# An attention stage's entries listed one by one, W_o split without GpSimd and late, and the last output on two queues

## The chip, the core and the metric

The kernel runs on one core of one Trainium2 chip. The metric is the device time of one execution in microseconds; the time before is the median of three runs. One execution was also taken by the hardware profiler, and all lines of the profile and the trace come from it.

## The reference

A decoder trunk of two layers over 256 positions of width 1024, in fp32. Layer 0 mixes positions with a gated linear recurrence, layer 1 with attention. Around each mixer stand two SwiGLU blocks of inner width 2816, and every part ends in a normalisation and a residual sum. The change touches layer 1's attention and the kernel's last output:

```python
q = (xq @ w_q).reshape(Bn, S, N_HEADS, HEAD_DIM).transpose(0, 2, 1, 3) * (HEAD_DIM ** -0.5)
for blk in range(S // Q_BLOCK):            # two blocks of 128 queries
    logits = jnp.einsum('bhqd,bhkd->bhqk', q[:, :, q0:end], k[:, :, :end])
    logits = logits + c[:, :, q0:end, None] - c[:, :, None, :end]
    logits = jnp.where(kpos[None, :] <= qpos[:, None], logits, -jnp.inf)
    p = jax.nn.softmax(logits, axis=-1)
    outs.append(jnp.einsum('bhqk,bhkd->bhqd', p, v[:, :, :end]))
...
return o @ w_o
...
h = h + rms_norm(m, mix_post_g[layer])
f = swiglu(rms_norm(h, ffn2_pre_g[layer]), ffn2_w_gate[layer], ffn2_w_up[layer], ffn2_w_down[layer])
h = h + 0.5 * rms_norm(f, ffn2_post_g[layer])
```

There are 16 heads of 64. The first block of queries looks at 128 keys, the second at 256.

## The kernel before

The 256 positions are two tiles of 128, t=0 and t=1. The residual stream `h[t]` stays in the core's memory; the weights are streamed from device memory once. TensorE (PE) follows the order of the program. The other engines, VectorE (DVE), ScalarE (ACT), GpSimd (POOL) and the DMA queue of SyncE (SP), get their order from a planner that works ahead of the run; `tc.high_priority()` favours instructions, and `tc.keep_in_program_order` pins one at its place in the program.

**Products in three passes.** Each fp32 operand is held as a high part in the format fp32r and a rest. `mm3` (lines 185 to 187) multiplies high by high, high by rest and rest by high into one PSUM bank.

**Units.** Weights come in units of 128 x 1024 numbers (512 KB). `load_raw` issues the transfer on SP's queue into one of five `raw` buffers; `split` makes `whi` (a cast) and `wlo` (raw minus `whi`), each with nine buffers. Normally ACT casts (line 174) and DVE subtracts (line 179). For every second unit of W_o (`dve=True`, odd k), DVE casts (line 172) and POOL subtracts.

**Items, slots and ticks.** `items` lists the units in the order of use, each with `prep` (load and split) and `work(t, u)` (the products of one tile). `slot(t, i)` runs the work and then a `tick`. A tick runs deferred steps that are due (`defer(n, fn)` waits for n further ticks) and calls `prepare_next`, which emits the load and split of the next unit, if the unit nine places earlier is finished by both tiles and an estimate of the transfer allows it. `half(t, i)` is a slot that afterwards sets `state["a"]` (t=0) or `state["b"]` (t=1) to the number of items that the tile has passed.

**The attention stage** begins at item `n_ffn3`: eight units of W_q (two column halves n of four units each), then eight of W_o (k = 0 to 7). A slot of either is six matmuls of 128x512. At the end of a column half, `heads_T` scales q into `htok` (DVE, line 921); two ticks later PE transposes it (line 926), and ACT (line 929) and DVE (line 930) each copy half of the heads into `qT`. Two more rows of `qT` come by small transfers on POOL's queue (`att_rows`, lines 914 and 915), which also loads the table for the exponential.

`attention(t)` works in groups of heads: four groups of four heads for t=0, eight groups of two for t=1. Each group has four operations:

- `logits`: matmuls (line 1030), then mask and maximum on DVE (1031, 1033), then exponentials with their sum on ACT (1038)
- `norm`: reciprocal and scaling of the probabilities `pe` on DVE (1044, 1045)
- `turn`: four transposes on PE (1051), copy to `pT` on ACT (1053)
- `values`: eight matmuls (1065); after each half of the heads, `oh` on ACT (1071) and `ol` on DVE (1072)

They are put together in steps: step i holds norm(i−1), logits(i), values(i−3) and turn(i−2). The order of the stage is written out by hand in `ATT_ORDER`: "0" or "1" is a slot of that tile, "a0" or "a1" the next step of that tile's attention. W_o's products for t=0 stand between the steps of t=1. After the last W_o slot, `enter` adds the normalised result to `h[t]` and prepares the input of the SwiGLU block that follows.

**The end.** `enter(..., last=True)` finishes the last block. For t=1 it cuts `h` into four pieces of 256 columns: three are one DVE instruction each (line 286) and leave on SP's queue; the first is scaled on ACT (288), added on POOL (289) and leaves on ACT's queue (line 291 issues all).

Of the kernel before, what the change touches and what calls it, by code (L numbers as in the profile page):

```python
# [9 lines left out]
F32 = mybir.dt.float32  # L10
F32R = mybir.dt.float32r
BF16 = mybir.dt.bfloat16
AF = mybir.ActivationFunctionType
ALU = mybir.AluOpType
# [30 lines left out]
def trunk_kernel(ctx: ExitStack, tc: tile.TileContext, A: dict, out: bass.AP):  # L45
# [108 lines left out]
    def load_raw(src, parts, n, pieces=1):  # L154
        v = new_raw()[:parts, :n]
        if len(src.shape) == 3:
            a, m = src.shape[1] // pieces, n // pieces
            for c in range(pieces):
                nc.sync.dma_start(v[:, c * m:(c + 1) * m].rearrange("p (a b) -> p a b", a=a),
                                  src[:, c * a:(c + 1) * a, :])  # L160
        else:
            nc.sync.dma_start(v, src)
        return v

    def split(rawv, parts, n, pieces=1, dve=False):
        u = Unit()
        hi = wpool.tile([P, 1024], F32R, tag="whi", name=nm("whi"), bufs=WB)
        lo = wpool.tile([P, 1024], F32R, tag="wlo", name=nm("wlo"), bufs=WB)
        m = n // pieces
        for c in range(0, n, m):  # L170
            if dve:
                nc.vector.tensor_copy(hi[:parts, c:c + m], rawv[:, c:c + m])
            else:
                up = nc.scalar.activation(hi[:parts, c:c + m], rawv[:, c:c + m], AF.Copy)  # L174
                if settled[0]:
                    tc.keep_in_program_order(up)
                    settled[0] = False
            low = nc.gpsimd if dve else nc.vector
            low.tensor_tensor(lo[:parts, c:c + m], rawv[:, c:c + m], hi[:parts, c:c + m].bitcast(F32), ALU.subtract)  # L179
        u.hi, u.lo = hi[:parts, :n], lo[:parts, :n]  # L180
        return u

# [78 lines left out]
    def enter(t, dests, pf, gb, half, last=False, normed=False):  # L261

        f = 1.0 / 16 if half else 1.0 / 32
        ss = new_ss()
        t1 = []
        urgent = tc.high_priority()
        urgent.__enter__()
        for n in range(2):
            square_sum(pf[n], ss[:, n:n + 1], f)
        for n in range(2):  # L270
            if n == 1 and last:
                r = rstd_of(ss, 2, f, nc.vector)
            t1.append(hpool.tile([P, 512], F32, tag="t1", name=nm("t1"), bufs=2))
            nc.vector.tensor_tensor(t1[n], pf[n], gb[:, n * 512:(n + 1) * 512], ALU.mult)  # L274
        if not last:
            r = rstd_of(ss, 2, f)

        ve, po, sp, aq = nc.vector, nc.gpsimd, nc.sync, nc.scalar
        pieces = [(n * 512, 512, ve, None) for n in range(2)]
        if last:  # L280
            pieces = ([(0, 256, ve, sp), (256, 256, ve, sp), (512, 512, ve, sp)] if t == 0 else
                      [(0, 256, po, aq), (256, 256, ve, sp), (512, 256, ve, sp), (768, 256, ve, sp)])
        for c, m, en, q in pieces:
            hn, tn = h[t][:, c:c + m], t1[c // 512][:, c % 512:c % 512 + m]
            if en is ve:
                en.scalar_tensor_tensor(hn, tn, r[:, 0:1], hn, ALU.mult, ALU.add)
            else:
                nc.scalar.activation(tn, tn, AF.Copy, scale=r[:, 0:1])
                en.tensor_tensor(hn, tn, hn, ALU.add)
            if last:  # L290
                q.dma_start(out[0, t * P:(t + 1) * P, c:c + m], hn)
        urgent.__exit__(None, None, None)
        if last:
            return

        def inputs():
            tps = [to_tp(h[t], n) for n in range(2)]
            for dest in dests:
                to_x(tps, dest)
            stat(t)  # L300

        def norm():
            with tc.high_priority():
                normed_x()

        def normed_x():
            ss = new_ss()
            for n in range(2):
                square_sum(h[t][:, n * 512:(n + 1) * 512], ss[:, n:n + 1])
            rs[t] = rstd_of(ss, 2)  # L310
            hn = []
            for n in range(2):
                hn.append(hpool.tile([P, 512], F32, tag="t1", name=nm("hn"), bufs=2))
                nc.vector.tensor_scalar(hn[n], h[t][:, n * 512:(n + 1) * 512], rs[t][:, 0:1], None, ALU.mult)

            def go():
                tps = []
                for n in range(2):
                    tp = gtbank()
                    for j in range(4):  # L320
                        nc.tensor.transpose(tp[:, j * P:(j + 1) * P], hn[n][:, j * P:(j + 1) * P], ident)
                    tps.append(tp)
                to_x_tiles(tps, dests[0])
            defer(6, go)

        if normed:
            norm()
            settled[0] = True
        else:
            defer(3, inputs)  # L330
# [14 lines left out]
    first_acc = []  # L345
    landed = {}

    def prepare_next(must=False):

        i = state["p"]  # L350
        if i >= len(items) or i >= WB and done.get(i - WB, 0) < 2:
            assert not must, i
            return
        if i not in landed:
            landed[i] = max(landed.get(i - 1, 4.0) + LOAD, pace["t"] if i < RAW else split_at[i - RAW] + LATE)
        if landed[i] > pace["t"] and not must:
            return
        pace["t"] = max(pace["t"], landed[i])
        split_at[i] = pace["t"] + 1.0
        units[i] = items[i][0]()  # L360
        state["p"] += 1
# [77 lines left out]
                    post(t, acc[t][:, :nn], acc[t][:, nn:2 * nn])  # L439
            items.append((prep, work))  # L440

    def row_items(w, widths, get_x, post, rows=2, dve=False, rows0=2):

        acc = {}
        kept = [[], []]
        nk = len(widths)
        r0 = 0
        for k, kp in enumerate(widths):  # L450
            def prep(kp=kp, r0=r0, k=k):
                return split(load_raw(w[r0:r0 + kp, :], kp, D), kp, D, dve=dve and k % 2 == 1)

            def work(t, u, k=k):
                if k == 0:
                    acc[t] = [mmbank(), mmbank()]
                m = rows if t == 1 else rows0
                if k >= nk - m:
                    kept[t].append((k, u))
                    if k < nk - 1:  # L460
                        return
                    todo = [(kk, uu, n) for n in range(2) for (kk, uu) in kept[t]]
                else:
                    todo = [(k, u, n) for n in range(2)]
                for (kk, uu, n) in todo:
                    mm3(acc[t][n], *get_x(t, kk), uu.hi[:, n * 512:(n + 1) * 512], uu.lo[:, n * 512:(n + 1) * 512],
                        kk == 0, kk == nk - 1)
                if k == nk - 1:
                    post(t, acc[t])
            items.append((prep, work))  # L470
            r0 += kp
# [545 lines left out]
    def attention(t):  # L1017
# [53 lines left out]
                nc.scalar.activation(oh_v, box["po"], AF.Copy)  # L1071
                nc.vector.tensor_tensor(ol_v, box["po"], oh_v.bitcast(F32), ALU.subtract)

        steps = []
        for i in range(G + 3):
            s = []
            if 0 <= i - 1 < G:
                s.append(lambda i=i: norm(i - 1))
            if i < G:
                s.append(lambda i=i: logits(i))  # L1080
            if 0 <= i - 3 < G:
                s.append(lambda i=i: values(i - 3))
            if 0 <= i - 2 < G:
                s.append(lambda i=i: turn(i - 2))
            steps.append(s)
        return steps

    def post_q(n):
        return lambda t, ps: heads_T(pools["a"], ps, t, n, HD ** -0.5, att["q"][t])

    for n in range(2):
        proj_items(A["attn_w_q"][0], n * 512, 512, main_x, post_q(n))
    n_q = len(items)
    row_items(A["attn_w_o"][0], [P] * 8, lambda t, k: (att["oh"][t][:, k, :], att["ol"][t][:, k, :]),
              lambda t, accs: enter(t, [main_dest(GI[("ffn2", 1)], t)], accs, gbox["mix1"], False), dve=True, rows0=1)
    ahead(n_q + 2, load_gb("mix1", A["mix_post_g"][1]))
    n_att = len(items)


    ffn_items(lambda: pools["f"], A["ffn2_w_gate"][1], A["ffn2_w_up"][1], A["ffn2_w_down"][1], A["ffn2_post_g"][1],  # L1100
              lambda t: None, last=True)

    ATT_ORDER = ("0 0 0 0 0 0 0 0 a0 1 a0 1 1 1 a0 1 a0 1 1 a0 1 a0 a1 a0 "
                 "0 a1 0 a1 0 a1 0 a1 0 a1 0 a1 0 a1 0 a1 1 a1 1 a1 1 1 1 1 1 1")


    def half(t, i):
# [163 lines left out]
    steps = [attention(0), attention(1)]  # L1271
    nxt = [n_ffn3, n_ffn3]
    for c in ATT_ORDER.split():
        if c[0] == "a":
            with tc.high_priority():
                for s in steps[int(c[1])].pop(0):
                    s()
        else:
            half(int(c), nxt[int(c)])
            nxt[int(c)] += 1  # L1280
    assert nxt == [n_att, n_att] and not steps[0] and not steps[1]
    acm.__exit__(None, None, None)

    fcm = open_pool("f", "ffn_c")
# [36 lines left out]
```

## Time and profile before

| | us |
|---|---|
| median of three runs | 1003.27 |
| lowest, highest run | 1002.89, 1005.62 |
| the profiled execution's own time | 1005.15 |
| its span, first to last instruction | 1003.4 |
| PE busy | 991.3 |
| DVE busy | 622.7 |
| ACT busy | 532.7 |
| POOL busy | 58.4 |

The time around the span, 1005.15 − 1003.4, belongs to the execution but not to any instruction of the profile. Busy PE means that some matmul is under way; matmuls overlap, and the granted clock (1.00 is full speed) tells how fast they run. In the rows of a group stand the line, engine, operation, result and operands, shape and count, then busy time, mean ns of one, and idle time before them. An arrow after an idle time names what ended it. In the timeline's rows stand start, length, engine, line and instruction.

### The profile page before, as it was taken

How to read it: one execution, taken by the hardware profiler on the slowest of the kernel's cores; microseconds unless marked ns; L12 is line 12 of the kernel's file. 1: busy time of each engine (PE TensorE's matmuls, PEld its weight loads, DVE VectorE, ACT ScalarE, POOL GpSimd, SP SyncE). 2: the span in 40 equal slices, each digit the busy share in tenths (PEclk: the TensorE clock that was granted, in tenths of full speed). 3: DMA queues.
4: the chain of work that ended last, by engine and by line, in shares of the span. 5: the costliest groups of instructions: out<-in, count | busy, mean ns of one | idle time of the engine just before them, and what ended most of it. 6: DMA issues, size and time to landing. Idle time of an engine off the chain costs nothing.

```text
span 1003.4 us, 12912 instructions
## 1 busy us (share of the span) xinstructions
PE 991.3 (99%) x4776; PEld 823.4 (82%) x4776; DVE 622.7 (62%) x791; ACT 532.7 (53%) x750; POOL 58.4 (6%) x97
## 2 busy tenths in 40 slices
PE   9999999999999999999999999999998999999997
PEld 6888888899988888888898888888886788888886
DVE  6756554668997555554786655554587675555542
ACT  7545443569976544443654444443464665444431
POOL 2400000100003000000100000000032000000000
PEclk9999999999999999999999999999998999999999
DMA  8867556565346766556467566655554067665531
GB/s 286 308 193 207 187 183 191 173 178 147 124 126 205 211 188 187 189 189 189 125 213 226 174 188 186 187 178 188 164 175 141 4 204 213 182 193 185 182 119 42
DMA packets 92645, 178.89 MB, mean 178 GB/s; under 512 B 11966, under 2 KB 32614, under 8 KB 92582
## 3 DMA queue, kind: packets, MB, share of 16 engines
q1 hardware_dynamic: 91142, 177.02, 57.5%
q10 hardware_dynamic: 608, 0.93, 0.3%
q8 instruction: 37, 0.61, 0.3%
q0 software_dynamic: 832, 0.12, 0.1%
q14 instruction: 26, 0.21, 0.1%
HBM read 176.95 MB, written 1.05 MB: 177 GB/s over the span
## 4 chain that ended last, share of the span: by engine, by line
PE 95%; DVE 2%; issue 1%; DMA 1%; ACT 0%; POOL 0%; DVEq 0%; ACTq 0%; POOLq 0%
PE mm L185 28%; PE mm L187 28%; PE mm L186 28%; PE tr L511 2%; PE gt L739 2%; PE mm L192 1%; PE mm L194 1%; PE mm L193 1%; PE gt L1030 1%; PE mm L1169 1%; PE gt L216 1%; DMA raw<-in_ffn_w_gate_dram 1%; PE mm L1065 1%; PE tr L1051 1%; DVE pe L1045 1%
## 5 line engine op out<-in xcount | busy, mean ns | idle before, releaser
L179 DVE TENSOR_TENSOR wlo<-raw,whi 128x1024 fp32r<-128x1024 f32 (+4 forms) x325 | 390.4, 1207 | 269.0 <-ACT whi L174 266.4
L174 ACT ACTIVATE whi<-raw 128x1024 fp32r<-128x1024 f32 (+4 forms) x325 | 337.8, 1045 | 314.4 <-PE mm L187 252.1
L185 PE MATMUL mm<-whi,xhi 128*128 128x512 f32 (+2 forms) x768 | 304.1, 396 | 0.0
L187 PE MATMUL mm<-whi,xlo 128*128 128x512 f32 (+2 forms) x768 | 298.8, 389 | 0.0
L186 PE MATMUL mm<-wlo,xhi 128*128 128x512 f32 (+2 forms) x768 | 298.1, 388 | 0.0
L187 PEld LDWEIGHTS mm<-whi,xlo 128*128 128x128 f32 x768 | 144.2, 188 | 30.3 <-DVE xlo L251 0.3
L186 PEld LDWEIGHTS mm<-wlo,xhi 128*128 128x128 f32 x768 | 144.4, 188 | 28.0 <-DVE wlo L179 0.3
L185 PEld LDWEIGHTS mm<-whi,xhi 128*128 128x128 f32 x768 | 144.3, 188 | 27.6
L185 PE MATMUL mm<-whi,hhi 128*128 128x512 f32 x352 | 139.1, 395 | 0.0
L187 PE MATMUL mm<-whi,hlo 128*128 128x512 f32 x352 | 137.8, 391 | 0.0
L186 PE MATMUL mm<-wlo,hhi 128*128 128x512 f32 x352 | 136.9, 389 | 0.0
L187 PEld LDWEIGHTS mm<-whi,hlo 128*128 128x128 f32 x352 | 66.1, 188 | 14.9
L186 PEld LDWEIGHTS mm<-wlo,hhi 128*128 128x128 f32 x352 | 66.1, 188 | 14.1
L185 PEld LDWEIGHTS mm<-whi,hhi 128*128 128x128 f32 x352 | 66.2, 188 | 13.1
L505 DVE SCALAR_TENSOR_TENSOR prod<-mm,rstd,sil 128x512 f32<-128x512 f32 (+1 forms) x48 | 33.8, 705 | 38.0 <-PE mm L187 34.3
L496 ACT ACTIVATE sil<-mm,rstd 128x512 f32<-128x512 f32 (+1 forms) x48 | 31.2, 652 | 40.4 <-PE mm L187 40.4
L200 POOL TENSOR_SCALAR nv<-ss 128x1 f32<-128x1 f32 x22 | 11.0, 502 | 705.3 <-ACT junk L207 705.3
L515 ACT ACTIVATE hhi<-tr 128x512 fp32r<-128x512 f32 (+1 forms) x48 | 26.6, 555 | 15.7 <-PE tr L511 15.6
L274 DVE TENSOR_TENSOR t<-mm,gb 128x512 f32<-128x512 f32 x24 | 16.2, 685 | 25.4 <-ACT junk L207 25.4
L516 DVE TENSOR_TENSOR hlo<-tr,hhi 128x512 fp32r<-128x512 f32 (+1 forms) x48 | 30.5, 642 | 1.4
L207 ACT ACTIVATE junk<-mm 128x512 bf16<-128x512 f32 x24 | 14.3, 597 | 31.4 <-PE mm L187 31.3
L185 PE MATMUL mm<-whi,zhi 128*128 128x340 f32 (+2 forms) x80 | 28.3, 354 | 0.0
(197 smaller groups left out, 936.6 us busy)
## 6 DMA issues: line engine op xcount, KB each, us to landing
raw<-in_ffn_w_down_dram SPq DMA_DIRECT2D x88, 512.0 KB
raw<-in_ffn_w_up_dram SPq DMA_DIRECT2D x80, 512.0 KB
raw<-in_ffn_w_gate_dram SPq DMA_DIRECT2D x78, 512.0 KB
raw<-in_rg_w_in_dram SPq DMA_DIRECT2D x20, 504.0 KB
raw<-in_rg_w_out_dram SPq DMA_DIRECT2D x10, 504.0 KB
raw<-in_ffn_w_gate_dram SPq DMA_DIRECT2D x18, 256.0 KB
raw<-in_ffn_w_up_dram SPq DMA_DIRECT2D x16, 256.0 KB
raw<-in_w_kv_dram SPq DMA_DIRECT2D x8, 512.0 KB
```

The source lines that it names most:

```text
L174: up = nc.scalar.activation(hi[:parts, c:c + m], rawv[:, c:c + m], AF.Copy)
L179: low.tensor_tensor(lo[:parts, c:c + m], rawv[:, c:c + m], hi[:parts, c:c + m].bitcast(F32), ALU.subtract)
L185: nc.tensor.matmul(ps, xh, wh, start=first, stop=False)
L186: nc.tensor.matmul(ps, xh, wl, start=False, stop=False)
L187: nc.tensor.matmul(ps, xl, wh, start=False, stop=last)
L274: nc.vector.tensor_tensor(t1[n], pf[n], gb[:, n * 512:(n + 1) * 512], ALU.mult)
L496: nc.scalar.activation(s[:, :nn], ps, AF.Silu, scale=rs[t][:, 0:1])
L505: nc.vector.scalar_tensor_tensor(pr[:, :nn], ps, rs[t][:, 0:1], s, ALU.mult, ALU.mult)
L511: nc.tensor.transpose(tp[:, j * P:(j + 1) * P], pr[:, j * P:(j + 1) * P], ident)
L515: nc.scalar.activation(hv, tp[:, :nn], AF.Copy)
L516: nc.vector.tensor_tensor(lv, tp[:, :nn], hv.bitcast(F32), ALU.subtract)
L739: nc.tensor.matmul(ps[:w, j * S:(j + 1) * S], wv[:, o:o + w], xc[:w, k, :], start=k == 0, stop=k == m - 1)
```

## The change

- `split` loses its parameter `dve`. All units, W_o's odd ones too, are cast on ACT and subtracted on DVE. A new parameter `pin` pins the cast in program order; `row_items` sets it for W_o's k above 3 (`late=True`).
- `prepare_next` does not prepare units `n_q + 4` to `n_q + 7` (W_o's k = 4 to 7) before `state["a"]` is at most three items short of them; since units are prepared in order, those behind wait with them. `n_q` is a list so that the function can read it.
- `attention(t)` returns the four operations as four lists. `ATT_ORDER` names each: l, n, t, v for logits, norm, turn and values, with the tile. The order for t=0 is new; t=0's first logits stand before the eighth slot of t=0, and t=1's first two logits ahead of W_o. In the steps of t=1 the order norm, logits, values, turn remains.
- In the last `enter`, t=1's four pieces are all DVE instructions, and leave on SP, ACT, SP and ACT.

```diff
-    def split(rawv, parts, n, pieces=1, dve=False):
+    def split(rawv, parts, n, pieces=1, pin=False):
...
-            if dve:
-                nc.vector.tensor_copy(hi[:parts, c:c + m], rawv[:, c:c + m])
-            else:
-                up = nc.scalar.activation(hi[:parts, c:c + m], rawv[:, c:c + m], AF.Copy)
-                if settled[0]:
-                    tc.keep_in_program_order(up)
-                    settled[0] = False
-            low = nc.gpsimd if dve else nc.vector
-            low.tensor_tensor(lo[:parts, c:c + m], rawv[:, c:c + m], hi[:parts, c:c + m].bitcast(F32), ALU.subtract)
+            up = nc.scalar.activation(hi[:parts, c:c + m], rawv[:, c:c + m], AF.Copy)
+            if settled[0] or pin:
+                tc.keep_in_program_order(up)
+                settled[0] = False
+            nc.vector.tensor_tensor(lo[:parts, c:c + m], rawv[:, c:c + m], hi[:parts, c:c + m].bitcast(F32), ALU.subtract)
...
-            pieces = ([(0, 256, ve, sp), (256, 256, ve, sp), (512, 512, ve, sp)] if t == 0 else
-                      [(0, 256, po, aq), (256, 256, ve, sp), (512, 256, ve, sp), (768, 256, ve, sp)])
-        for c, m, en, q in pieces:
+            pieces = ([(0, 256, sp), (256, 256, sp), (512, 512, sp)] if t == 0 else
+                      [(0, 256, sp), (256, 256, aq), (512, 256, sp), (768, 256, aq)])
+        for c, m, q in pieces:
             hn, tn = h[t][:, c:c + m], t1[c // 512][:, c % 512:c % 512 + m]
-            if en is ve:
-                en.scalar_tensor_tensor(hn, tn, r[:, 0:1], hn, ALU.mult, ALU.add)
-            else:
-                nc.scalar.activation(tn, tn, AF.Copy, scale=r[:, 0:1])
-                en.tensor_tensor(hn, tn, hn, ALU.add)
+            nc.vector.scalar_tensor_tensor(hn, tn, r[:, 0:1], hn, ALU.mult, ALU.add)
             if last:
                 q.dma_start(out[0, t * P:(t + 1) * P, c:c + m], hn)
...
+    n_q = [1 << 20]
+    near = 3
+
     def prepare_next(must=False):
         i = state["p"]
         if i >= len(items) or i >= WB and done.get(i - WB, 0) < 2:
             assert not must, i
+            return
+        if n_q[0] + 3 < i < n_q[0] + 8 and state["a"] < i - near and not must:
             return
...
-                return split(load_raw(w[r0:r0 + kp, :], kp, D), kp, D, dve=dve and k % 2 == 1)
+                return split(load_raw(w[r0:r0 + kp, :], kp, D), kp, D, pin=late and k > 3)
...
-        steps = []
-        for i in range(G + 3):
-            s = []
-            if 0 <= i - 1 < G:
-                s.append(lambda i=i: norm(i - 1))
-            if i < G:
-                s.append(lambda i=i: logits(i))
-            if 0 <= i - 3 < G:
-                s.append(lambda i=i: values(i - 3))
-            if 0 <= i - 2 < G:
-                s.append(lambda i=i: turn(i - 2))
-            steps.append(s)
-        return steps
+        return {c: [lambda i=i, f=f: f(i) for i in range(G)] for c, f in zip("lntv", (logits, norm, turn, values))}
...
-    ATT_ORDER = ("0 0 0 0 0 0 0 0 a0 1 a0 1 1 1 a0 1 a0 1 1 a0 1 a0 a1 a0 "
-                 "0 a1 0 a1 0 a1 0 a1 0 a1 0 a1 0 a1 0 a1 1 a1 1 a1 1 1 1 1 1 1")
+    ATT_ORDER = ("0 0 0 0 0 0 0 l0 0 1 n0 l0 1 t0 1 n0 1 l0 v0 t0 1 n0 l0 1 v0 t0 n0 1 l1 v0 t0 1 n1 l1 v0 0 "
+                 "n1 l1 t1 0 n1 l1 v1 t1 0 n1 l1 v1 t1 0 n1 l1 v1 t1 0 n1 l1 v1 t1 0 n1 l1 v1 t1 0 n1 v1 t1 0 "
+                 "v1 t1 1 v1 1 1 1 1 1 1 1")
...
-        if c[0] == "a":
+        if c[0] in "lntv":
             with tc.high_priority():
-                for s in steps[int(c[1])].pop(0):
-                    s()
+                steps[int(c[1])][c[0]].pop(0)()
```

More of the change, by code (lines that the diff above doesn't have):

```diff
@@ L276, in enter @@
             r = rstd_of(ss, 2, f)
-        ve, po, sp, aq = nc.vector, nc.gpsimd, nc.sync, nc.scalar
-        pieces = [(n * 512, 512, ve, None) for n in range(2)]
+        sp, aq = nc.sync, nc.scalar
+        pieces = [(n * 512, 512, None) for n in range(2)]
         if last:
-            pieces = ([(0, 256, ve, sp), (256, 256, ve, sp), (512, 512, ve, sp)] if t == 0 else
-                      [(0, 256, po, aq), (256, 256, ve, sp), (512, 256, ve, sp), (768, 256, ve, sp)])
-        for c, m, en, q in pieces:
+            pieces = ([(0, 256, sp), (256, 256, sp), (512, 512, sp)] if t == 0 else
+                      [(0, 256, sp), (256, 256, aq), (512, 256, sp), (768, 256, aq)])
+        for c, m, q in pieces:
             hn, tn = h[t][:, c:c + m], t1[c // 512][:, c % 512:c % 512 + m]
-            if en is ve:
-                en.scalar_tensor_tensor(hn, tn, r[:, 0:1], hn, ALU.mult, ALU.add)
-            else:
-                nc.scalar.activation(tn, tn, AF.Copy, scale=r[:, 0:1])
-                en.tensor_tensor(hn, tn, hn, ALU.add)
+            nc.vector.scalar_tensor_tensor(hn, tn, r[:, 0:1], hn, ALU.mult, ALU.add)
             if last:
@@ L440, in pair_items, with row_items @@
             items.append((prep, work))
-    def row_items(w, widths, get_x, post, rows=2, dve=False, rows0=2):
+    def row_items(w, widths, get_x, post, rows=2, rows0=2, late=False):
         acc = {}
@@ L1092, in trunk_kernel @@
         proj_items(A["attn_w_q"][0], n * 512, 512, main_x, post_q(n))
-    n_q = len(items)
+    n_q[0] = len(items)
     row_items(A["attn_w_o"][0], [P] * 8, lambda t, k: (att["oh"][t][:, k, :], att["ol"][t][:, k, :]),
-              lambda t, accs: enter(t, [main_dest(GI[("ffn2", 1)], t)], accs, gbox["mix1"], False), dve=True, rows0=1)
-    ahead(n_q + 2, load_gb("mix1", A["mix_post_g"][1]))
+              lambda t, accs: enter(t, [main_dest(GI[("ffn2", 1)], t)], accs, gbox["mix1"], False), rows0=1, late=True)
+    ahead(n_q[0] + 2, load_gb("mix1", A["mix_post_g"][1]))
     n_att = len(items)
@@ L1280, in trunk_kernel @@
             nxt[int(c)] += 1
-    assert nxt == [n_att, n_att] and not steps[0] and not steps[1]
+    assert nxt == [n_att, n_att] and not any(s for st in steps for s in st.values())
     acm.__exit__(None, None, None)
```

## Prediction

> **What bounds the kernel now.** I read the page's busy shares first, then the waits of TensorE (PE), then a table of three stretches around the attention, then PE's timeline in them.
>
> ```profile
> span 1003.4 us, 12912 instructions
> PE 991.3 (99%) x4776; PEld 823.4 (82%) x4776; DVE 622.7 (62%) x791; ACT 532.7 (53%) x750; POOL 58.4 (6%) x97
> ```
>
> PE's stream of matmuls is the kernel. A change that removes no matmul can win only where PE waits or runs slowly, and the next row, from the waits of PE, holds nearly all its idle time between the first and the last matmul.
>
> ```profile
> PE tr L1051 <- DVE pe L1045: 4.5, 2, 2.8
> ```
>
> Two waits, 4.5 us, both of `turn`'s transposes for VectorE's (DVE) normalisation `pe` in the attention. The table by stretches (length; busy time of PE, PEld, DVE, ACT, POOL; granted clock; DMA share; GB/s) shows what stands around them:
>
> ```profile
> 742.60:766.40 23.80, 19.39 (x125) 15.75 (x124) 22.93 (x30) 12.90 (x42) 9.50 (x4) 1.00 0.46 133
> 766.40:773.90 7.50, 7.42 (x27) 5.60 (x27) 3.74 (x6) 2.11 (x6) 0.00 (x0) 0.54 0.49 140
> 773.90:796.00 22.10, 22.10 (x142) 17.02 (x141) 13.56 (x28) 11.34 (x36) 0.00 (x0) 1.00 0.00 1
> ```
>
> In the first stretch (t=0's attention beside t=1's q products) DVE is busy 22.93 of 23.80 us: there DVE is the bound. The second follows the longer wait: PE is never idle, but its granted clock is 0.54. In the third (t=1's attention beside W_o of t=0) PE runs without a gap, while DVE has 22.10 − 13.56 = 8.5 us free and ACT 10.8.
>
> PE's timeline (start, duration, line; the two waits in brackets, then one undisturbed step of the third stretch):
>
> ```profile
> 758.74 0.66 PE L1065 MATMUL mm<-pT,v 128*64 128x128 f32 x8
> 761.05 0.63 PE L1051 MATMUL tr<-ident,pe 128*128 128x128 f32 x4 [1.65 <-DVE pe L1045]
> ...
> 762.98 0.66 PE L1065 MATMUL mm<-pT,v 128*64 128x128 f32 x8
> 766.48 1.03 PE L1051 MATMUL tr<-ident,pe 128*128 128x128 f32 x4 [2.84 <-DVE pe L1045]
> ...
> 773.83 0.59 PE L185 MATMUL mm<-whi,oh 128*128 128x512 f32 x1
> ...
> 782.91 0.66 PE L1065 MATMUL mm<-pT,v 128*64 128x128 f32 x8
> 783.49 0.66 PE L1051 MATMUL tr<-ident,pe 128*128 128x128 f32 x4
> 783.91 0.47 PE L185 MATMUL mm<-whi,oh 128*128 128x512 f32 x1
> ...
> 785.37 1.03 PE L1030 MATMUL gt<-kT,qT 66*128 66x256 f32 x4
> 786.33 0.66 PE L1065 MATMUL mm<-pT,v 128*64 128x128 f32 x8
> 786.91 0.66 PE L1051 MATMUL tr<-ident,pe 128*128 128x128 f32 x4
> ```
>
> From start to start an undisturbed step takes 0.96 us for logits (785.37 to 786.33), 0.58 for values, 0.42 for the transposes (783.49 to 783.91) and 1.46 for a slot of six products (783.91 to 785.37). So the first wait costs 761.05 − 758.74 − 0.58 = 1.73 us, the second 766.48 − 762.98 − 0.58 = 2.92. From 766.48 to 773.83 PE did transposes, logits, values, one slot and logits again: 0.42 + 0.96 + 0.58 + 1.46 + 0.96 = 4.38 us of work in 7.35, so the slow clock cost 2.97. Together **7.6 us** are to be had here, and that is the ceiling of the attention part.
>
> **W_o's splits.** DVE by operation and shape in 742.6 to 766.4 (count, then busy us and mean ns):
>
> ```profile
> L1045 DVE TENSOR_TENSOR pe<-pe,sm 128x512 f32<-128x512 f32 x4 | 7.5, 1880 | 0.0
> L179 DVE TENSOR_TENSOR wlo<-raw,whi 128x1024 fp32r<-128x1024 f32 x4 | 4.8, 1210 | 0.0
> L172 DVE CAST whi<-raw 128x1024 fp32r<-128x1024 f32 x4 | 2.7, 682 | 0.0
> ```
>
> Its rows for the maximum and the normalisation in the third stretch, and ACT's cast in the first:
>
> ```profile
> L1033 DVE TENSOR_REDUCE mx<-gt 128x2 f32<-128x512 f32 x7 | 4.8, 690 | 0.2
> L1045 DVE TENSOR_TENSOR pe<-pe,sm 128x512 f32<-128x512 f32 x6 | 4.1, 690 | 0.2
> L174 ACT ACTIVATE whi<-raw 128x1024 fp32r<-128x1024 f32 x4 | 4.3, 1063 | 1.5 <-PE mm L187 1.5
> ```
>
> The same normalisation takes 1880 ns where GpSimd (POOL) has its four subtractions (9.50 us busy) and 690 where it has none. Without POOL: 7.5 − 4 × 0.69 = 4.7 us less on DVE. The four casts go to ACT: 2.7 less on DVE, 4 × 1.06 more on ACT. The four subtractions come to DVE: 4 × 1.21 = 4.8 more. That alone is 2.6 us less, which would only shorten the 4.65 us of waits. The late split does the rest. Before, this stretch holds DVE subtractions of W_o's k=2, 4, 6 and of the next FFN's first unit. After, units k=4 to 7 may be prepared only once t=0 has finished k−3, and since the count rises after a slot's tick, k=4's split stands behind k=1's products, in the third stretch. The first stretch keeps k=1 to 3, 3 × 1.21 = 3.6 instead of 4.8 + 4.8. DVE there: 22.93 − 4.7 − 2.7 − 4.8 (prior subtractions) + 3.6 = 14.3 us, and at most 2 × 2 × 0.69 = 2.8 for mask and maximum of two groups of t=1's logits that come by then. Some 17 of the 23.80 − 4.65 = 19.2 us that the stretch takes without its waits, and more with the slot and the logits that it gains, no longer bound PE. **I take both waits and the slow clock as gone: −7.6.**
>
> By the Trainium skill ("TensorE: Matmul & The Clock Gate", Part 1: The HAM clock gate) the clock halves after an idle window of about 3.4 us and returns after about 3.4 us of sustained work. By that, an estimate of the loss here would be half of 3.4, 1.7 us, and the part would bring 6.3. The trace differs on both: a wait of 2.84 us sufficed and the low clock held for 7.5 us, so the measured 2.97 stands.
>
> **What becomes late instead.** The moved splits land on the third stretch: k=4 to 7 and the FFN's first unit, 5 × 1.21 = 6.05 us on DVE against 8.5 free, 5 × 1.06 = 5.3 on ACT against 10.8. PE's slack there:
>
> ```profile
> 782.57 0.69 DVE L1045 TENSOR_TENSOR pe<-pe,sm 128x512 f32<-128x512 f32 x1
> 787.67 0.60 ACT L1053 ACTIVATE pT<-tr 128x512 f32<-128x512 f32 x1 [1.97 <-PE tr L1051]
> 789.75 0.66 PE L1065 MATMUL mm<-pT,v 128*64 128x128 f32 x8
> ```
>
> The probabilities that are normalised at 783.26 are transposed at 786.91 (the transposes between belong to the group before): 3.65 us to spare, against one cast and two subtractions in the way, 3.5. `pT` ends at 788.27, its values start at 789.75: 1.5 to spare against one cast of 1.06. I take **0**, bounds 0 and 2.27 (one cast and one subtraction) in each of five steps. W_o's weights need no haste: k=4 is used two slots behind its split. The DMA issues of these units move with them, still in the same order on SP; the third stretch moves 1 GB/s, so the queue has room, and nothing on it is overtaken. The gate also holds back the FFN's first unit, behind k=7, but the others already wait for t=1's W_o to free their buffers.
>
> **The list.** One entry per operation adds no instruction; it moves some. t=0's first logits come one slot earlier. What they read:
>
> ```profile
> 737.51 0.49 POOL L915 DMA_DIRECT2D qT<-mone  x1
> qT<-mone POOLq DMA_DIRECT2D x2, 8.0 KB, 3.8
> 740.70 0.69 DVE L930 COPY qT<-tr 64x512 f32<-64x512 f32 x1 [1.39 <-ACT qT L929]
> 741.27 0.40 PE L185 MATMUL mm<-whi,xhi 128*128 128x512 f32 x1
> ```
>
> PE would reach them at 741.27, where the last slot now begins. The copy ends at 741.39, the row lands at 737.51 + 3.8 = 741.3. Cost 0 to 0.4, I take **0.2**. t=1's first logits get closer to their heads:
>
> ```profile
> 756.82 0.60 PE L926 MATMUL tr<-ident,htok 128*128 128x128 f32 x4
> 762.07 0.69 DVE L930 COPY qT<-tr 64x512 f32<-64x512 f32 x1
> ```
>
> After, PE comes to them behind these transposes, values, transposes and one slot: 0.42 + 0.58 + 0.42 + 1.46 = 2.9 us. Before, the copy ended 5.9 us after them, on the full DVE. With room, this copy needs 0.69 and ACT's half of it, which goes first, about as much; exponentials may stand ahead on ACT. 0 to 1.0, I take **0.5**. For the rest of t=0's steps a single subtraction of 1.21 may get in front of one chain: 0 to 1.2, I take **0.5**. W_o of t=1 starts with fewer attention entries beside it; `enter` of t=0 loses about one slot of its lead, hidden behind the slots that follow.
>
> **Last output.** The end of the timeline (the first row counts the first two of the second's three pieces):
>
> ```profile
> 998.84 0.88 DVE L286 SCALAR_TENSOR_TENSOR h<-t,rstd,h 128x256 f32<-128x256 f32 x2
> 998.84 1.75 DVE L286 SCALAR_TENSOR_TENSOR h<-t,rstd,h 128x256 f32<-128x256 f32 x3
> 999.42 0.88 POOL L289 TENSOR_TENSOR h<-t,h 128x256 f32<-128x256 f32 x1 [0.62 <-ACT t L288]
> 1000.33 0.35 ACTq L291 DMA_DIRECT2D out_dram<-h  x1
> ```
>
> DVE's first two pieces take 0.88 us, the third, beside POOL's addition, as long again, and ends at 1000.59. Four pieces at 0.44 end at 998.84 + 1.76 = 1000.6 as well, and the last issue leaves from ACT instead of SP. I take **0**, bounds −0.2 and +0.3.
>
> **Sum.** −7.6 + 0.2 + 0.5 + 0.5 = −6.4 us. The profiled execution took 1005.15 us (span 1003.4, 1.75 around it): 998.75. The median of the runs, 1003.27, is 1.88 lower; I forecast medians: **996.9**. Its own range: everything gained, 1003.27 − 7.8 = 995.5, to all small costs at their upper bound, −7.6 + 0.4 + 1.0 + 1.2 + 0.3 = −4.7, 998.6.
>
> **The rivals.** *t=1's heads come late.* If the copy for t=1's first logits keeps its 5.9 us, PE waits 5.9 − 2.9 = 3.0 us there, as long as the wait that brought the slow clock, with 2.97 more: 7.6 − 6.0 = 1.6 gained, 1001.7. For it: that is where the copy stood, and a plan made ahead may keep it there. Against: DVE's work there falls from 22.9 to some 17 us.
>
> *The late split does nothing,* because the planner keeps these splits early. Then DVE drops by 2.6 us alone; 2.0 us of wait stay, and if the slow clock stays as well the gain is 2.6, 1000.7. Against it: the casts are now pinned in program order.
>
> *Slower: the splits cramp t=1's steps.* Place: ACT and DVE from t=0's W_o k=2 on. A pinned cast holds ACT's queue, behind it exponentials and `pT`, on which values wait; the subtraction then stands ahead of mask and maximum. If cast and subtraction show in full in all five steps, 5 × 2.27 = 11.35 − 7.6 = 3.7 lost, 1007.0. It ends even from 7.6 / 5 = 1.5 us per step, and the slacks of 3.65 and 1.5 us speak against it; for it speaks that 3.5 of those 3.65 could be used up.
>
> **How the numbers follow.** 0.3% of 1003.27 is 3.0 us, about what a measurement here can tell from no change. Forecast 0.71; late heads 0.14; late split idle 0.05; cramped steps 0.10. Late heads and an idle split fall within 0.3% for the most part, parts of each on either side: faster 0.73, same 0.16, slower 0.11. The range reaches from 995.2 (everything gained, and the 0.4 by which the fastest run lies below the median) to late heads, 1001.7.
>
> **What would show it.** Right: no PE wait for `pe` above 0.5 us, clock 1.00 through the stage, normalisations of about 690 ns, no POOL subtraction, DVE below 80% in t=0's part. Wrong: a stretch at a clock near 0.54 in 740 to 800, a PE wait of logits for `qT`, steps of t=1 longer than 3.42 us (782.91 to 786.33 from values to values), or values that wait for `pT`.

## The result and the profile after

| | before | after |
|---|---|---|
| median of five runs, us | 1003.27 | 998.18 |
| lowest, highest run | 1002.14, 1005.62 | 997.55, 999.82 |
| profiled execution, its span | 1005.15, 1003.4 | 998.38, 996.7 |

The ratio is 0.9945, with a 95% interval from 0.9926 to 0.9963. The forecast was 996.9, with a range from 995.2 to 1001.7. Executions of before differ with their mean granted clock: of the 37 that were taken beside the experiments, the eight at 0.998 or 0.999 took 1001.9 to 1004.3 us and the 24 at 0.996 or less 1004.4 to 1006.8, while the five of after stand at 0.998 or 0.999.

To tell the stage from the scatter of the runs, take one length from PE's timeline: from the last transposes of `h` ahead of the attention to the first product of the last SwiGLU block (its operand is `xhi` again). First the two rows of before, then those of after:

```profile
723.96 1.03 PE L216 MATMUL gt<-ident,h 128*128 128x128 f32 x8
810.70 0.39 PE L185 MATMUL mm<-whi,xhi 128*128 128x512 f32 x1
```

```profile
724.17 1.03 PE L212 MATMUL gt<-ident,h 128*128 128x128 f32 x8
742.55 1.13 PE L1027 MATMUL gt<-kT,qT 66*128 66x128 f32 x8 [0.91 <-DMA qT<-mone]
804.09 0.40 PE L181 MATMUL mm<-whi,xhi 128*128 128x512 f32 x1
```

The stage took 86.74 us and takes 79.92: 6.82 less. What is left of the span is 1003.4 − 86.74 = 916.66 before and 996.7 − 79.92 = 916.78 after. So the whole gain lies in this stage, and the output on two queues is worth nothing that shows. The row between is the only PE wait that is left there: t=0's first logits wait for a row of `qT`.

The three stretches of the prediction, at the same times of the trace after (length; busy time of PE, PEld, DVE, ACT, POOL; clock; DMA share; GB/s):

```profile
742.60:766.40 23.80, 23.80 (x152) 19.59 (x153) 18.33 (x31) 13.80 (x47) 0.00 (x0) 1.00 0.23 67
766.40:773.90 7.50, 7.50 (x46) 6.04 (x45) 6.02 (x12) 5.50 (x14) 0.00 (x0) 1.00 0.00 0
773.90:796.00 22.10, 22.10 (x144) 16.52 (x144) 17.96 (x31) 16.39 (x40) 1.12 (x4) 1.00 0.41 120
```

PE is busy throughout, the clock is 1.00, and DVE went from 22.93 to 18.33 us in the first stretch and from 13.56 to 17.96 in the third. The groups on DVE in the first stretch, and its subtractions in the third:

```profile
L175 DVE TENSOR_TENSOR wlo<-raw,whi 128x1024 fp32r<-128x1024 f32 x3 | 3.6, 1214 | 0.0
L1042 DVE TENSOR_TENSOR pe<-pe,sm 128x512 f32<-128x512 f32 x5 | 3.4, 689 | 0.1
```

```profile
L175 DVE TENSOR_TENSOR wlo<-raw,whi 128x1024 fp32r<-128x1024 f32 x6 | 7.3, 1221 | 1.3 <-ACT whi L171 1.3
```

The normalisation takes 689 ns instead of 1880; three subtractions are left in t=0's part, as forecast, and a fifth normalisation has come into the stretch, as PE is further on at the same time.

### The profile page after: what moved, and what is told of

Same layout as the page of the kernel before. It is cut to its first block, busy times and chain, and to the rows that moved or that the text cites. A ratio compares the mean times of both kernels' runs of the same rounds, so it can differ in the third digit from the quotient of the medians.

```text
span 996.7 us, 12904 instructions
## 1 busy us (share of the span) xinstructions
PE 987.9 (99%) x4776; PEld 821.1 (82%) x4776; DVE 619.2 (62%) x792; ACT 535.8 (54%) x753; POOL 47.6 (5%) x92
## 3 DMA queue, kind: packets, MB, share of 16 engines
HBM read 176.95 MB, written 1.05 MB: 179 GB/s over the span
## 4 chain that ended last, share of the span: by engine, by line
PE 95%; DMA 1%; issue 1%; DVE 1%; POOL 0%; ACT 0%; POOLq 0%; DVEq 0%; ACTq 0%
PE mm L181 28%; PE mm L183 28%; PE mm L182 28%; PE tr L508 2%; PE gt L736 2%; PE gt L1027 1%; PE mm L188 1%; PE mm L190 1%; PE mm L189 1%; PE mm L1155 1%; PE mm L1062 1%; PE tr L1048 1%; DMA raw<-in_ffn_w_gate_dram 1%; PE gt L212 1%; DMA qT<-mone 0%
## 5 line engine op out<-in xcount | busy, mean ns | idle before, releaser
L175 DVE TENSOR_TENSOR wlo<-raw,whi 128x1024 fp32r<-128x1024 f32 (+4 forms) x329 | 395.3, 1207 | 270.0 <-ACT whi L171 267.3
L171 ACT ACTIVATE whi<-raw 128x1024 fp32r<-128x1024 f32 (+4 forms) x329 | 342.0, 1045 | 312.9 <-PE mm L183 250.9
```

The source lines that it names most:

```text
L175: nc.vector.tensor_tensor(lo[:parts, c:c + m], rawv[:, c:c + m], hi[:parts, c:c + m].bitcast(F32), ALU.subtract)
```

## The experiments

All runs by the length of the stage, from their profiled executions (start and end from the same two PE rows). The rest of the span is 916 to 918 us in every one of them. Each length is that of one execution; the kernel after, taken twice, gave 79.92 and 79.85.

| run | what differs | stage, us | span |
|---|---|---|---|
| before | | 810.70 − 723.96 = 86.74 | 1003.4 |
| after | | 804.09 − 724.17 = 79.92 | 996.7 |
| e1 | before, W_o without POOL | 804.80 − 724.46 = 80.34 | 997.5 |
| e2 | e1, and split late | 803.88 − 724.59 = 79.29 | 996.4 |
| e3 | before, new order | 813.34 − 724.61 = 88.73 | 1006.1 |
| e4 | e1, new order | 805.52 − 724.41 = 81.11 | 998.1 |
| e5 | after, first logits a slot later | 804.53 − 724.13 = 80.40 | 997.1 |
| e6 | after, rows of qT due earlier | 804.25 − 724.96 = 79.29 | 996.8 |
| e7 | before, odd units all on DVE | 805.01 − 724.26 = 80.75 | 997.7 |
| e8 | before, odd units cast on ACT | 804.11 − 724.31 = 79.80 | 996.8 |
| e9 | after, transposes one slot behind | 808.45 − 724.25 = 84.20 | 1001.0 |
| e10 | after, transposes right behind | 808.85 − 724.24 = 84.61 | 1001.4 |
| e11 | after, rows of qT due at once | 802.58 − 723.76 = 78.82 | 995.1 |
| e12 | after again | 803.54 − 723.69 = 79.85 | 996.1 |

### The parts one by one

**e1: POOL taken out.**

```diff
-              ..., gbox["mix1"], False), dve=True, rows0=1)
+              ..., gbox["mix1"], False), rows0=1)
```

> The kernel before, W_o's odd units cast on ACT and subtracted on DVE; order, gate and output as before. The stretch from the last transposes ahead of the attention (723.96) to the first product of the last SwiGLU block (810.70) took 86.74 us before and 79.92 after. Theory (an overfull DVE makes the waits): DVE loses 2.6 us in t=0's part, normalisations fall from 1880 ns to about 690, waits for them shrink from 4.5 us to about 2 and the stretch by 2.6 to 5.6 us. Rival (the order alone makes the waits): both waits stay near 1.7 and 2.8 us with the slow clock, the stretch stays within 1 us of 86.7.

Median 999.48 of four runs, ratio 0.9942 (0.992 to 0.9964). Its one PE wait in the stage, and its first stretch:

```profile
763.70 0.63 PE L1051 MATMUL tr<-ident,pe 128*128 128x128 f32 x4 [1.52 <-DVE pe L1045]
```

```profile
742.60:766.40 23.80, 22.28 (x147) 18.17 (x146) 21.50 (x31) 17.80 (x49) 0.00 (x0) 1.00 0.47 135
```

The stage falls by 6.40 us, more than the upper end of what was expected, though DVE is still busy 21.50 of 23.80 us. One wait of the two is gone; the other, 1.52 us, left the clock at 1.00. This part alone holds nearly the whole gain.

**e2: and split late.** The order string of after is replaced by the old steps, written as single entries.

> The kernel after, but with the operations of the attention in the order of before (written as single entries). POOL is gone from W_o and k=4 to 7 are split late. Theory (overfull DVE): no wait for the normalisation over 0.5 us, clock 1.00, the stretch that took 86.74 us before and 79.92 after takes 79 to 80. Rival (order): at least one of the two waits stays, 83 us or more.

Median 998.1 of four, ratio 0.9929 (0.9903 to 0.9955).

```profile
760.20 0.63 PE L1048 MATMUL tr<-ident,pe 128*128 128x128 f32 x4 [0.45 <-DVE sm L1041]
```

The late split brings 1.05 us more, and the old order does better here than the new one in the kernel after (79.29 against 79.92).

**e3: the order alone.** Before, with the new `ATT_ORDER` and the four lists.

> The kernel before with the new order of the attention alone; W_o's odd units still on DVE and POOL, nothing split late, output as before. Theory (overfull DVE): t=0's part stays above 90% DVE busy, normalisations beside POOL's work take over 1.5 us, waits of 2 us or more stay, the stretch (86.74 before, 79.92 after) takes 84 to 88 us. Rival (order): the waits go, 80 to 82 us, the wait of 0.9 us for the rows of qT among them.

Median 1008.68 of ten, ratio 1.0035 (1.0022 to 1.0048): slower. PE's waits in the stage:

```profile
743.00 1.13 PE L1030 MATMUL gt<-kT,qT 66*128 66x128 f32 x8 [0.92 <-DMA qT<-mone]
750.75 0.63 PE L1051 MATMUL tr<-ident,pe 128*128 128x128 f32 x4 [1.17 <-ACT qT L929]
757.52 0.63 PE L1051 MATMUL tr<-ident,pe 128*128 128x128 f32 x4 [1.92 <-DVE pe L1045]
764.23 0.63 PE L1051 MATMUL tr<-ident,pe 128*128 128x128 f32 x4 [1.40 <-DVE pe L1045]
770.38 1.08 PE L1051 MATMUL tr<-ident,pe 128*128 128x128 f32 x4 [2.69 <-DVE pe L1045]
```

The order gains nothing by itself: three waits for the normalisation instead of two, and two new ones. The 88.73 us lie above the 84 to 88 of the expectation. Behind the wait of 2.69 the clock fell:

```profile
770.00:772.00 2.00, 1.62 (x6) 1.55 (x7) 0.84 (x2) 0.50 (x2) 0.00 (x0) 0.50 0.50 117
772.00:774.00 2.00, 2.00 (x7) 1.56 (x7) 0.19 (x1) 1.20 (x6) 0.00 (x0) 0.66 0.38 145
```

**e4: order and POOL, no gate.**

```diff
-    near = 3
+    near = 100
...
-              ..., rows0=1, late=True)
+              ..., rows0=1)
```

> The kernel after without the gate and without the pin: the new order, W_o split on ACT and DVE, as early as buffers allow. Theory (overfull DVE, with the late split a needed part): some wait of 0.5 to 2 us returns in t=0's part, the stretch (79.92 after) takes 80.5 to 82 us. Rival (the late split does nothing once POOL is gone): 79.7 to 80.2 us, no wait but that for the rows of qT.

Median 999.95 of five, ratio 0.9952 (0.9932 to 0.9972).

```profile
759.75 0.63 PE L1048 MATMUL tr<-ident,pe 128*128 128x128 f32 x4 [1.37 <-DVE pe L1042]
769.66 0.63 PE L1048 MATMUL tr<-ident,pe 128*128 128x128 f32 x4 [0.55 <-DVE sm L1041]
```

With e1 and e2 this makes a square: the gate is worth 80.34 − 79.29 = 1.05 us in the old order and 81.11 − 79.92 = 1.19 in the new; the new order costs 81.11 − 80.34 = 0.77 without the gate and 0.63 with it, and 1.99 beside POOL.

### Why POOL mattered

**e7: casts and subtractions of the odd units on DVE,** so that DVE is as full as before and POOL idle.

```diff
-            low = nc.gpsimd if dve else nc.vector
+            low = nc.vector
```

> The kernel before, with W_o's odd units cast and subtracted on DVE: POOL does nothing in the stage, DVE does four subtractions more and keeps its casts. By sum DVE is as full as before: 22.9 - 4.7 + 4.8 = 23.0 of 23.8 us. Theory one (POOL's work beside DVE slows the normalisations that PE waits for): they take about 690 ns, waits shrink to 1.5 to 2.5 us in all and no slow clock, the stretch (86.74 before, 80.34 with casts on ACT) takes 80.5 to 82.5 us. Theory two, the prediction's (DVE's load by sum makes the waits): 84 us or more.

Median 999.57 of four, ratio 0.9951 (0.9935 to 0.9967).

```profile
742.60:766.40 23.80, 22.35 (x147) 18.25 (x146) 22.61 (x34) 14.12 (x44) 0.00 (x0) 1.00 0.41 115
```

```profile
763.42 0.63 PE L1051 MATMUL tr<-ident,pe 128*128 128x128 f32 x4 [1.45 <-DVE pe L1045]
770.96 0.63 PE L1051 MATMUL tr<-ident,pe 128*128 128x128 f32 x4 [0.29 <-DVE pe L1045]
```

DVE is busy 22.61 of 23.80 us, as before, and the stage is 5.99 us shorter all the same. With DVE as full by sum, 1.74 of the 4.5 us of waits are left, the clock stays at 1.00, and the normalisations take 0.68 us again. So the load by sum did not make most of the loss.

**e8: casts on ACT, subtractions left on POOL.**

> The kernel before, with W_o's odd units cast on ACT, and still subtracted on POOL: DVE loses 2.7 us of casts (20.2 of 23.8 by sum), POOL's work beside it stays. Theory one (POOL's work slows the normalisations): they stay at 1.5 us or more where POOL works, waits of 2 us or more stay, 83 us or more. Theory two (DVE's load by sum): waits shrink as far as without POOL, 80 to 82 us.

Median 998.78 of four, ratio 0.9944 (0.9928 to 0.996). The expectation of theory one failed: POOL works as long as before, and yet no wait in the stage is over 0.35 us, and the stage is as short as after. The other theory's 80 to 82 us, by DVE's sum, is nearly met: DVE is busy 20.25 of 23.80 us here. So e8 alone doesn't tell the sum from the place of POOL's work; e7 speaks against the sum, and where POOL's work fell fits both runs. Before, DVE (cast, then normalisation) and POOL:

```profile
757.17 0.68 DVE L172 CAST whi<-raw 128x1024 fp32r<-128x1024 f32 x1
758.57 2.33 DVE L1045 TENSOR_TENSOR pe<-pe,sm 128x512 f32<-128x512 f32 x1
```

```profile
757.98 2.37 POOL L179 TENSOR_TENSOR wlo<-raw,whi 128x1024 fp32r<-128x1024 f32 x1 [4.21 <-PE tr L926]
```

In e8, a subtraction of DVE and one of POOL:

```profile
763.88 2.53 DVE L176 TENSOR_TENSOR wlo<-raw,whi 128x1024 fp32r<-128x1024 f32 x1
```

```profile
762.98 2.35 POOL L176 TENSOR_TENSOR wlo<-raw,whi 128x1024 fp32r<-128x1024 f32 x1 [5.16 <-ACT whi L171]
```

POOL's subtraction before ended at 760.35, and the normalisation at 760.90, 0.55 us later, about what it takes alone. In e8 POOL ended at 765.33 and DVE's subtraction at 766.41, 1.08 later, again about its own length. The DVE instruction did its work after POOL's, not beside it. All four normalisations of before and all four of e3 end 0.54 or 0.55 us behind a subtraction of POOL. Before, POOL could start only when DVE's cast had ended (in all four cases it started 0.07 to 0.13 us later, whatever its row names), and soon behind that cast on DVE stood a normalisation: the casts on DVE timed the collision. In e8 the cast comes from ACT. Of POOL's four subtractions there, two meet a DVE subtraction, one meets a normalisation (1.39 us, and PE does not wait for it), and one meets neither. That this shift, and not the 2.7 us less on DVE, freed PE in e8 is argued from these rows, not shown by a run of its own. By the Trainium skill ("SBUF — State Buffer", SBUF: two separate sides) the port pair that VectorE and GpSimd share is an exclusive lock that the first holds for its whole instruction, and a VectorE instruction with two SBUF inputs needs it; the 0.55 and 1.08 us agree.

### The wait at the first logits

**e5: the first logits behind the eighth slot again.**

```diff
-    ATT_ORDER = ("0 0 0 0 0 0 0 l0 0 1 n0 l0 1 ...
+    ATT_ORDER = ("0 0 0 0 0 0 0 0 l0 1 n0 l0 1 ...
```

> The kernel after with one entry moved: t=0's first logits stand behind the eighth slot of t=0 again, as before. Theory (the new place asks for the rows of qT before their transfer lands): the wait of 0.91 us goes, the stretch from the transposes to the last SwiGLU block falls from 79.92 to 78.8 to 79.0 us, no PE wait is left in the stage, about 1 us faster than the kernel after. Rival (the wait only moves down the chain, as logits now come a slot later): a wait of 0.5 to 1 us for qT or for a normalisation appears, the stretch stays at 79.7 or more.

Median 999.54 of six, ratio 0.995 (0.9935 to 0.9964).

```profile
749.41 0.63 PE L1048 MATMUL tr<-ident,pe 128*128 128x128 f32 x4 [1.45 <-DVE pe L1042]
```

The rival was right: the early place had given the first normalisation a slot of lead, and without it the first transposes wait longer than the logits did.

**e6 and e11: the rows earlier.**

```diff
-    defer(6, att_rows)
+    defer(3, att_rows)
```

This is e6; e11 has `defer(0, att_rows)` there, and e12 is the kernel after, unchanged.

> The kernel after with the small transfers for qT's rows (and the table load beside them) deferred by three ticks instead of six; the order is untouched. Theory (the transfer's landing makes the wait): they are issued some 3 to 4 us earlier, the wait for them goes, and at most 0.2 us for the copy of qT stays: 78.8 to 79.1 us. Rival (POOL's queue is held by the normalisation's small operations, or the table load delays ACT): a wait of 0.5 us or more stays at the first logits, 79.5 us or more.

> The kernel after with the transfers for qT's rows and the table load due at the first tick of the stage, so that they stand ahead of the last two small normalisation operations on POOL's queue. Theory: they are issued 4 us or more earlier and landed long before the first logits, no PE wait over 0.2 us is left in the stage, which takes 78.8 to 79.0 us instead of 79.92; about 1 us, 0.1%, faster than the kernel after in the same call. Rival (POOL's pinned transfers or the early table load delay the normalisation of t=1's input, which the q products read): a wait of 0.5 us or more appears ahead of 740 us, and nothing is gained.

> The kernel after, unchanged, on the same chip as its neighbour for a direct comparison: stage 79.9 us with its wait of 0.9 us for the rows of qT, if that wait belongs to the order; a wait under 0.4 us if it came from one slow transfer.

The first logits, and POOL's issue of the row, in e6 (one run, 998.53):

```profile
742.72 1.13 PE L1027 MATMUL gt<-kT,qT 66*128 66x128 f32 x8 [0.29 <-DMA qT<-mone]
```

```profile
738.51 0.48 POOL L912 DMA_DIRECT2D qT<-mone  x1
```

In e11 (median 998.14 of five, ratio 0.9933, 0.992 to 0.9947):

```profile
741.07 1.11 PE L1027 MATMUL gt<-kT,qT 66*128 66x128 f32 x8
```

```profile
732.86 0.48 POOL L912 DMA_DIRECT2D qT<-mone  x1
```

In e12 (median 998.86 of six, ratio 0.9945, 0.9933 to 0.9958):

```profile
742.02 1.13 PE L1027 MATMUL gt<-kT,qT 66*128 66x128 f32 x8 [0.85 <-ACT warm L909]
```

In e6 POOL's queue issued the row no earlier, counted from the stage's start (738.51 − 724.96 = 13.55 us): the small operations of the normalisation ahead of it held it, as the rival said. Only the table load moved, and the wait shrank to 0.29; the stage's 79.29 us lie between the two expectations. In e11 the row left at 732.86 − 723.76 = 9.10 and no wait is left; the stage is 1.03 us shorter than that of e12 beside it. e12's wait ends with the table load's dummy activation, by its row; whether the table load held PE itself or slowed the landing stays open. e11 is the fastest kernel here by its stage. Its median lies 0.7 us below e12's, and the intervals overlap: against the kernel after, the runs do not settle it.

### The slow clock

**e9 and e10: one long wait, nothing before it.** The first transposes stand one slot (e9) or none (e10) behind the first logits.

> The kernel after, but t=0's first logits stand behind the eighth slot and the first transposes follow one slot later, ahead of the second logits; so PE waits once, for the first normalisation, and for nothing before it. Floor of the stage without a wait: some 78.9 us. Theory one (a single wait as long as the second of before, 2.84 us, brings the slow clock): wait of 2.3 to 3.0 us, granted clock near 0.5 for some 7 us behind it, 3 us more, stretch 84 to 85 us. Theory two (it needs two waits close together, 1.65 and 2.84 us within 8 us as before): the wait alone, clock 1.00, 81.2 to 82 us.

> As the other kernel of this call, with no slot between the first logits and the first transposes: one wait of 3.6 to 4.2 us. Theory one (a single wait of 2.8 us or more brings the slow clock): clock near 0.5 for some 7 us behind it, stretch 85.5 to 86.5 us. Theory two (two waits close together are needed): clock 1.00, 82.5 to 83.3 us.

One run each, 1002.73 and 1003.16. The wait of e9 and the stretches behind it, then the same for e10:

```profile
748.95 0.88 PE L1048 MATMUL tr<-ident,pe 128*128 128x128 f32 x4 [3.57 <-DVE pe L1042]
```

```profile
748.00:750.00 2.00, 1.05 (x6) 1.08 (x7) 0.77 (x2) 0.14 (x1) 0.00 (x0) 0.80 0.55 127
750.00:752.00 2.00, 2.00 (x10) 1.90 (x9) 0.43 (x1) 0.46 (x1) 0.00 (x0) 0.50 0.33 135
752.00:754.00 2.00, 2.00 (x11) 1.58 (x11) 0.96 (x2) 0.48 (x1) 0.00 (x0) 0.85 0.00 0
```

```profile
748.12 1.08 PE L1048 MATMUL tr<-ident,pe 128*128 128x128 f32 x4 [4.14 <-DVE pe L1042]
```

```profile
746.00:748.00 2.00, 0.00 (x0) 0.00 (x0) 0.87 (x2) 1.04 (x6) 0.00 (x0) 0.97 0.00 0
748.00:750.00 2.00, 1.88 (x7) 1.71 (x8) 0.00 (x0) 0.60 (x1) 0.00 (x0) 0.50 0.00 0
750.00:752.00 2.00, 2.00 (x10) 1.67 (x9) 0.00 (x0) 0.35 (x1) 0.00 (x0) 0.67 0.00 0
```

A single wait of 3.57 us, or of 4.14, brought the slow clock, so at that length two close together are not needed. It holds for about 3.4 us in each: in e9, 0.8 + 2 + 0.6 us at half speed give the means 0.80, 0.50 and 0.85, and in e10 and e3 the rows give about as much. At half speed 3.4 us cost 1.7: with e11's stage, which has no wait, that makes 78.82 + 3.57 + 1.7 = 84.1 us for e9 and 78.82 + 4.14 + 1.7 = 84.7 for e10, where 84.20 and 84.61 were measured. The 7 us of the expectations did not come back. Both waits were longer than the 2.84 us of before. The shortest wait with a slow clock behind it is e3's 2.69, the longest without one e3's 1.92; but before and e3 had other waits some us ahead, and whether 2.7 us alone suffice no run shows.

## Why the prediction was right, and where not

**The size of what was to be had** was right. With no wait at all (e11) the stage takes 7.92 us less than before; the prediction's sum of two waits and the slow clock was 7.6. The 0.3 between them are the slow clock, which the prediction put at 2.97: the 2 us rows at the end of this text give 6.8 us at half speed (the 7.5 of the prediction is the width of its window), so 3.4 lost, and 1.65 + 2.84 + 3.4 = 7.9.

**That both waits and the slow clock go** was right, and so were the signs named for it: no wait for `pe`, clock 1.00, normalisations of 689 ns, DVE below 80% in t=0's part (18.33 of 23.80). One sign of being wrong came too, logits that wait for `qT`, 0.91 us, though at t=0's heads and not at those of t=1 that the rival was about.

**The cause was sized wrongly.** The step "That alone is 2.6 us less, which would only shorten the 4.65 us of waits. The late split does the rest" failed. Without POOL alone the stage fell by 6.40 us, and the late split added 1.05 to 1.2. The rival of an idle late split, priced at a gain of 2.6, would have gained 5.63 (e4). The error was to price waits by DVE's sum of work: e7 keeps the sum (22.61 us) and only 1.74 us of the waits, as the normalisation no longer stands behind POOL's instruction. The two errors, too little for POOL and too much for the gate, cancelled in the total; that the total came out is luck to this extent.

**The third stretch** was costed at 0, and no wait came. The spare time shrank as its bounds allowed:

```profile
782.80 0.68 DVE L1042 TENSOR_TENSOR pe<-pe,sm 128x512 f32<-128x512 f32 x1
```

```profile
785.77 0.66 PE L1048 MATMUL tr<-ident,pe 128*128 128x128 f32 x4
```

From the end of a normalisation, 783.48, to its transposes are now 2.3 us, where 3.65 had been. A step of t=1 still takes 3.42 us (781.77 to 785.19 from values to values), so the rival of cramped steps was far from its point of decision.

**The list** was given 0.2, 0.5 and 0.5 us for three places. The first cost 0.91 of wait, more than its bound of 0.4; at the second, t=1's heads, and in the rest of t=0's steps there was none. The sum, 1.2 forecast, came out near the measured one, 7.92 − 6.82 = 1.1; the places did not, so that was luck. The prediction left out that the row's landing time was only a median and that the table load stands on ACT at just this place.

**The total.** −6.4 forecast, −6.8 between the two profiled executions, −5.1 between medians. The profiled execution of before lay 1.9 us above its median, that of after 0.2; the ratio says 0.55%, 5.5 us. The measured 998.18 lies 1.3 above the forecast, inside the likeliest case's own range. Those 1.3 come from the step to medians: the forecast for the profiled execution, 998.75, was 0.4 too high, but the 1.88 us between profiled execution and median were carried over from before, and after has 0.2. Beside e12, with eleven executions of before, the medians lie 1005.02 − 998.86 = 6.2 apart. (By its own terms the lower end of the range is 995.1, not 995.2; nothing hangs on it.)

**The clock.** The rule of the Trainium skill ("TensorE: Matmul & The Clock Gate", Part 1: The HAM clock gate) that full speed returns after some 3.4 us of work agrees with e9, e10 and e3, and not with before, where half speed lasted 6.8 us. That it drops after an idle window of about 3.4 us fits e9 and e10 and not the others: it dropped behind waits of 2.84 us (before) and 2.69 (e3).

## What to carry to other kernels

When a DVE instruction takes two or three times its usual length, look at what POOL did at its start, and whether the long instruction ends one normal length after POOL's: then, as here, it was probably shut out, and it matters only if the shut-out instruction is one that others wait for. A sum of busy time on an engine tells that waits are possible, not how long they are; an experiment that keeps the sum and removes the collision separates the two. Before an order is rewritten to give operations more distance, try the old order with the collision removed: here it was as good or better.

## What the hardware showed that was not expected

The collision of DVE and POOL works both ways: in e8 one subtraction of POOL that started 0.22 us after a normalisation did took 2.73 us instead of 2.35 to 2.41. The slow clock held for 3.4 us after single waits and for 6.8 us before (766.56 to 773.4, from the clocks of 2 us stretches); what decides between the two was not found.

```profile
766.00:768.00 2.00, 1.52 (x6) 1.47 (x7) 1.47 (x2) 0.40 (x1) 0.00 (x0) 0.64 0.46 96
768.00:770.00 2.00, 2.00 (x11) 1.12 (x10) 0.72 (x2) 0.20 (x1) 0.00 (x0) 0.50 0.85 231
770.00:772.00 2.00, 2.00 (x8) 1.50 (x5) 1.24 (x3) 1.51 (x5) 0.00 (x0) 0.50 0.55 207
772.00:774.00 2.00, 2.00 (x8) 1.60 (x6) 0.71 (x2) 0.00 (x0) 0.00 (x0) 0.65 0.00 0
```
